# A hybrid decoder block in float32 parts: other rooms for w_out's first half rows, another order at the outset, and another closing norm

## The chip, the core and the metric

The kernel runs on one core of one Trainium2 chip. The metric is the device time of one execution in microseconds (us), lower is better. A core has a matrix engine (TensorE, in the profile PE for its products and PEld for its weight loads), a vector engine (VectorE, DVE), a scalar engine (ScalarE, ACT), a general engine (GpSimd, POOL) and a queue engine (SyncE, SP) that here only issues transfers. Each engine takes its own instructions in a fixed order. An instruction whose operand isn't there yet holds up all that stand behind it on the same engine, SP's transfers included.

## What is computed

One decoder block over 1024 tokens of width 1024, everything in float32:

```python
proj = x @ w_in                     # 1024 x 7168: q, f, i, out-gate, pool_v, gate_a, gate_b
a = HGRN2(q, f, i) -> per-head RMSNorm * sigmoid(og) -> @ w_a
b = per-group linear(causal_mean_w(pool_v) - pool_v) * pool_scale
mix = (sigmoid(gate_a) * a + sigmoid(gate_b) * b) @ w_out
x = LN(alpha * x + mix)
x = LN(alpha * x + relu(x @ w_up)**2 @ w_down)
```

`LN` takes a row's mean and variance over its 1024 columns, then multiplies by `g` and adds `b`.

## The kernel before, in words

**Products in three parts.** TensorE works on a rounded float32 format. Each operand is split into a high part (a cast on ScalarE) and a low part (a subtraction on VectorE), and a product is three matmuls of 128x128 by 128x512: high by high, high by low, low by high. Such a split of a weight row is `split` (L127, L128), of a weight block `w_part` (L250, L251), of an activation `split_into` (L132, L133), of a row of `w_out` `out_row` (L1181, L1182).

**Fewer products.** Every large product is cut into 2x2 blocks and done with seven block products instead of eight (names `a11`, `a12`, `s3`, `a22`, `s2`, `s1`, `s4` for the token operands, `p1` to `p7` for the products), with sums of blocks on VectorE before and after.

**Outset (L462 to L640).** SP first loads, in turns, 128-column pieces of `x`'s first 512 tokens (`load_x`, L488) and the rows of the first block `b11` of `w_in` (`load_block`, L505): pieces k=0, k=1, then k=2 and 3 together. TensorE runs `IDLE_PRODUCTS` = 12 products of the identity (L470), whose results nobody reads, then the transpose of the small parameters `prm` (L471, copied by L472). `first_tokens("a11")` transposes the sixteen 128x128 pieces of `x` (L171, four to a PSUM bank, one bank for each k), splits each bank into high and low (L132, L133) and copies it to `xt` (L188). `parts(b11)` splits the weight rows (L127, L128). Then `onto_chain` (L528 to L530) runs k by k, in each k over four banks `chain[c]`, the 48 matmuls of the first product; L561 copies the four banks away. The transposes of `a12`, the second half of `x`'s columns, stand between them, and `by_rows` follows with the next product (banks `ps_sc`, `ps_hg`).

**Rooms for loads in the stage of w_a.** The stage goes through two sets of two column pairs of `w_a` (`run(*(p[i : i + 1] for p in two))`). In the first set, `o_operand` (L672) loads each raw token operand into a 128x512 room got from `c_tile`: a ring of rooms named `c`, four in pool `ca`, and every third one in pool `wq`, which has two. `o_operand` is called for the seventh and last time ahead of the first set's sixth step of seven. In both sets `gated` (L1194 to L1198) loads two rows per result, a gate into one of ten rooms `ga` and a pooled row into one of two rooms `gb`. After the second set's second and third step, `out_rows_of` loads the eight half rows of `w_out` (columns 0 to 511), each through `loaded` (L660) into a room `gb` as well, and `out_row` splits it into an `act` tile. There are 28 `act` tiles; the split of `w_out`'s rows takes over those that the `a12` and `s3` token operands leave. L655 loads the other half rows of `w_out`. The product with `w_out` is `mix` (L114 to L116).

**End (from L1512).** The last block of the MLP's second product ends in two steps, `p3` (added to columns 512 to 1023, `nh` = 1) and `p2` (to columns 0 to 511, `nh` = 0), each over four row tiles c of 128 tokens, 12 matmuls a tile (L1492 to L1494). `add_to` (L1448) adds a finished bank onto the row tile on VectorE. `last_norm` then normalises it: for c < 3 with a sum on ScalarE (L1520, L1521), a sum of squares on ScalarE (L1522), a root (L1523), and on VectorE two passes over 1024 columns (L1528 multiplies by `g2`, L1531 multiplies by the reciprocal of L1529 and adds `b2`), and a transfer out (L1532). For c = 3, VectorE takes statistics of each half (L1260) and joins them (L1516), and both passes are cut into two halves, with a transfer each.

**What sets the order.** The kernel is written in a framework that traces it, then orders each engine's instructions by simulating the time, with program order as priority; `tc.high_priority(n)` raises it, and `tc.issue_after(ins)` puts an instruction behind `ins` in the order of its own engine, without a wait. A tile from a ring waits for the release of the tile that had the room. In one long stretch in the middle TensorE keeps program order; in the stages named above it doesn't.

Of the kernel before, what the change touches and what calls it, by code (L numbers as in the profile page):

```python
# [16 lines left out]
P = 128  # L17
S = 1024
D = 1024
# [23 lines left out]
IDLE_PRODUCTS = 12  # L43
# [9 lines left out]
def tile_hybrid_block(  # L53
# [36 lines left out]
    def nm(s):  # L90
        seq[0] += 1
        return f"{s}_{seq[0]}"
# [91 lines left out]
    def first_tokens(name, *tags):  # L184
        for kp in range(CH):
            ps, _ = transposed(r[:CH], HALF if name == "a12" else 0, kp, tags[kp % len(tags)])
            in_parts(name, kp, ps)
            A.copy(xt[name == "a12"][kp], ps)  # L188
# [272 lines left out]
    with tc.tile_pool(name="xr", bufs=8, side="right", reuse_waits="tile") as xr:  # L461
# [6 lines left out]

        for _ in range(IDLE_PRODUCTS):
            PE.matmul(ps[:, P : 2 * P], ident, ident, start=True, stop=True)  # L470
        PE.transpose(ps[:, 0:32], prm_r, ident[0:32, 0:32])  # L471
        V.tensor_copy(prm, ps[:, 0:32])  # L472
# [49 lines left out]
        def parts(rows):  # L522
            return [split(row, row_tile) for row in rows]
# [61 lines left out]
        first_tokens("a11", "tr", "tr", "hg", "hg")  # L585
        w = parts(b11[:2])
        for row, kp in zip(b11[2:], (1, 3)):
            lo_done, hi_done = made_kp["a11", kp]
            with tc.issue_after(lo_done), tc.issue_after(hi_done):
                w += parts([row])  # L590
# [11 lines left out]
        first_tokens("a12", "tr")  # L602
        onto_chain(w, "a11", True, copied(c11, c_late))
# [89 lines left out]
    with tc.tile_pool(name="tmp", bufs=1, side="right", reuse_waits="tile") as tmp:  # L693
# [527 lines left out]
        def out_rows_of(*ks):  # L1221
            for k in ks:
                out_row(loaded(w_out[k * P : (k + 1) * P, :HALF], mg_tile("gb", 2)), parts_of(act_tile))
# [288 lines left out]
    def last_norm(t):  # L1512

        mv = stat.tile([P, 4], F32, tag="lmv", name=nm("lmv"), bufs=4)
        if t == CH - 1:
            V.bn_aggr(mv[:, 0:2], st1[t])  # L1516
            A.activation(mv[:, 2:3], mv[:, 1:2], AF.Sqrt, bias=eps_ln)
        else:
            junk = dr.tile([P, D], F32, tag="junk", name=nm("junk"))
            A.activation(junk, r[t], AF.Copy, accum_out=mv[:, 3:4])  # L1520
            A.activation(mv[:, 0:1], mv[:, 3:4], AF.Copy, scale=-1.0 / D)  # L1521
            A.activation(junk, r[t], AF.Square, bias=mv[:, 0:1], accum_out=mv[:, 1:2])  # L1522
            A.activation(mv[:, 2:3], mv[:, 1:2], AF.Sqrt, bias=eps_ln, scale=1.0 / D)  # L1523
        n = 2 if t == CH - 1 else 1
        parts = [slice(i, i + D // n) for i in range(0, D, D // n)]
        for w in parts:
            op = ALU.subtract if t == CH - 1 else ALU.add
            V.scalar_tensor_tensor(r[t][:, w], r[t][:, w], mv[:, 0:1], g2[:, w], op, ALU.mult)  # L1528
        V.reciprocal(mv[:, 2:3], mv[:, 2:3])  # L1529
        for w, eng in zip(parts, (nc.sync, nc.scalar)):  # L1530
            V.scalar_tensor_tensor(r[t][:, w], r[t][:, w], mv[:, 2:3], b2[:, w], ALU.mult, ALU.add)  # L1531
            eng.dma_start(out=out2[t * P : (t + 1) * P, w], in_=r[t][:, w])  # L1532
# [37 lines left out]
    for i, c in ((0, 0), (0, 1), (1, 0), (0, 2), (1, 1), (1, 2), (0, 3), (1, 3)):  # L1570
        _, _, chain, fresh, (_, nh) = ends[i]
        ps = down_tile(ops[i], chain, fresh, c)
        with tc.high_priority(PRIO) if c == CH - 1 else nullcontext():
            add_to(c, nh, ps)
            if c == CH - 1:
                st1[c] = st1[c] if i else stat_tile()
                stats(r[c], nh, st1[c])
            if i:
                last_norm(c)
# [31 lines left out]
```

## Time and profile before

| | us |
|---|---|
| Median of 3 runs | 1447.27 |
| Lowest and highest of them | 1445.94, 1448.71 |
| The profiled execution's own time | 1449.68 |
| Its span, first to last instruction | 1447.9 |
| TensorE busy with products in the span | 1430.0 |
| VectorE, ScalarE, GpSimd busy | 1099.8, 757.6, 108.8 |

The profile is of one execution of its own, 2.41 us above the median of the three timed runs; 1.78 us of its time lie outside the span. A row of the timeline gives the start in us from the span's start, the duration, the engine, the line, the operation with out<-in, shapes and a count where equal instructions were merged, and in brackets the idle time of the engine before it with what ended it. Durations on TensorE overlap: a 128x512 product is shown with 0.39 us, but in a full stream one begins every 0.227 us. An SPq row is the issue of a transfer; its data arrive later.

### The profile page before, as it was taken

The page shows a single profiled execution, that of the slowest core. Times are in us where ns is not written, and L with a number is a line of the kernel's source. Part 1 is how long each engine was busy: PE and PEld are TensorE (multiplying, and loading weights), DVE is VectorE, ACT ScalarE, POOL GpSimd, SP SyncE. Part 2 cuts the span into 40 slices and gives each one's busy share as a digit, 9 for nine tenths or more (in the row PEclk, how much of TensorE's full clock was granted, in tenths as well). Part 3 has the DMA queues.
Part 4 walks back from the last instruction along what each step waited for, and adds up shares of the span by engine and source line. Part 5 has one row for each costly group of instructions (what it writes and reads, how often), then busy time and mean ns, then how long its engine had stood idle before and what let it go on. Part 6 is the DMA issues. An engine that isn't in the chain of part 4 may idle for free.

```text
span 1447.9 us, 20884 instructions
## 1 busy us (share of the span) xinstructions
PE 1430.0 (99%) x7377; PEld 1187.9 (82%) x7377; DVE 1099.8 (76%) x1807; ACT 757.6 (52%) x1383; POOL 108.8 (8%) x296
## 2 busy tenths in 40 slices
PE   9999999999999999999999999999999999999997
PEld 7888888888888888878788888888888888888886
DVE  5967877887797796579875697666666887777977
ACT  5445566666656645556433376555556443433535
POOL 0002011111212110100002100000000100000000
PEclk9999999999999999999999999999999999999999
DMA  7143254444444546799571225444457864445322
GB/s 269 61 137 94 84 131 145 109 126 145 110 124 132 136 126 190 211 318 321 173 245 62 88 73 189 160 160 157 143 174 254 289 244 148 149 145 173 118 72 117
DMA packets 186649, 228.15 MB, mean 158 GB/s; under 512 B 12176, under 2 KB 110512, under 8 KB 186544
## 3 DMA queue, kind: packets, MB, share of 16 engines
q1 hardware_dynamic: 179936, 210.81, 44.1%
q0 software_dynamic: 5824, 13.63, 4.5%
q10 hardware_dynamic: 784, 2.38, 0.6%
q8 instruction: 58, 0.95, 0.3%
q14 instruction: 47, 0.39, 0.1%
HBM read 149.70 MB, written 77.07 MB: 157 GB/s over the span
## 4 chain that ended last, share of the span: by engine, by line
PE 88%; DVE 6%; DMA 3%; issue 1%; ACT 1%; SPq 0%; DVEq 0%; ACTq 0%
PE ps_pj L213 15%; PE ps_pj L216 14%; PE ps_pj L215 14%; PE ps_pj L1493 4%; PE ps_pj L1494 4%; PE ps_pj L1492 4%; PE ps_pj L116 2%; PE ps_pj L115 2%; PE ps_pj L114 2%; PE ps_tr L1494 1%; PE ps_tr L1493 1%; PE ps_tr L1492 1%; DMA raw<-in_w_a_dram 1%; PE ps_hg L213 1%; PE ps_pj L529 1%
## 5 line engine op out<-in xcount | busy, mean ns | idle before, releaser
L213 PE MATMUL ps_pj<-act,w 128*128 128x512 f32 x1068 | 420.8, 394 | 4.4 <-ACT room L294 2.0
L215 PE MATMUL ps_pj<-act,w 128*128 128x512 f32 x1068 | 416.0, 390 | 0.0
L216 PE MATMUL ps_pj<-act,w 128*128 128x512 f32 x1068 | 415.9, 390 | 0.0
L250 ACT CAST w<-raw 128x512 fp32r<-128x512 f32 x303 | 187.6, 621 | 261.4 <-PE ps_pj L215 184.7
L251 DVE TENSOR_TENSOR w<-raw,w 128x512 fp32r<-128x512 f32 x303 | 206.9, 686 | 94.6 <-ACT w L250 93.0
L213 PEld LDWEIGHTS ps_pj<-act,w 128*128 128x128 f32 x1068 | 200.9, 188 | 48.7 <-DVE c L298 3.4
L216 PEld LDWEIGHTS ps_pj<-act,w 128*128 128x128 f32 x1068 | 200.9, 188 | 42.6
L215 PEld LDWEIGHTS ps_pj<-act,w 128*128 128x128 f32 x1068 | 200.9, 188 | 40.7
L1454 ACT CAST act<-act 128x1024 fp32r<-128x1024 f32 x66 | 66.9, 1050 | 110.1 <-issue 35.0
L1494 PE MATMUL ps_pj<-act,act 128*128 128x512 f32 x240 | 93.0, 389 | 0.0
L1493 PE MATMUL ps_pj<-act,act 128*128 128x512 f32 x240 | 93.0, 389 | 0.0
L1455 DVE TENSOR_TENSOR act<-act,act 128x1024 fp32r<-128x1024 f32 x66 | 79.4, 1219 | 17.5 <-ACT act L1454 16.5
L1492 PE MATMUL ps_pj<-act,act 128*128 128x512 f32 x240 | 92.5, 389 | 0.0
L298 DVE TENSOR_TENSOR c<-c,ps_pj 128x512 f32<-128x512 f32 x91 | 62.1, 682 | 34.4 <-PE ps_pj L216 33.6
L294 ACT COPY c<-ps_pj 128x512 f32<-128x512 f32 x92 | 53.5, 582 | 3.6 <-PE ps_pj L216 2.2
L1492 PEld LDWEIGHTS ps_pj<-act,act 128*128 128x128 f32 x240 | 45.0, 188 | 9.4
L1493 PEld LDWEIGHTS ps_pj<-act,act 128*128 128x128 f32 x240 | 45.0, 188 | 9.4
L1494 PEld LDWEIGHTS ps_pj<-act,act 128*128 128x128 f32 x240 | 45.0, 188 | 9.3
L303 DVE TENSOR_TENSOR raw<-raw,raw 128x512 f32<-128x512 f32 x43 | 29.6, 688 | 25.9 <-DMA raw<-in_w_in_dram 17.2
L1363 ACT ACTIVATE c<-c 128x512 f32<-128x512 f32 x61 | 38.6, 633 | 1.7
L1362 ACT ACTIVATE c<-c 128x512 f32<-128x512 f32 x46 | 29.1, 632 | 15.8 <-DVE c L298 15.8
L688 POOL DMA_DIRECT2D s<-og x28 | 25.0, 1164 | 138.7 <-DVE og L1105 138.7
(418 smaller groups left out, 2699.5 us busy)
## 6 DMA issues: line engine op xcount, KB each, us to landing
h<-c SPq DMA_DIRECT2D x106, 256.0 KB, 3.0
raw<-in_w_in_dram SPq DMA_DIRECT2D x100, 256.0 KB, 3.3
act<-h SPq DMA_DIRECT2D x78, 256.0 KB, 2.9
draw<-in_w_down_dram SPq DMA_DIRECT2D x16, 1024.0 KB, 7.9
raw<-in_w_up_dram SPq DMA_DIRECT2D x56, 256.0 KB, 3.0
hf<-h SPq DMA_DIRECT2D x34, 256.0 KB, 2.9
s<-og POOLq DMA_DIRECT2D x28, 256.0 KB, 6.2
v<-v SPq DMA_DIRECT2D x16, 256.0 KB, 3.3
```

The source lines that it names most:

```text
L213: PE.matmul(ps, wh[:, k], th, start=first and k == 0, stop=False, skip_group_check=True)
L215: PE.matmul(ps, wh[:, k], tl, start=False, stop=False, skip_group_check=True)
L216: PE.matmul(ps, wl[:, k], th, start=False, stop=k == CH - 1, skip_group_check=True)
L250: hi_of.append(A.copy(hi, src).ins)
L251: lo_of.append(V.tensor_sub(lo, src, f(hi)).ins)
L294: noted(A.copy(t, ps))
L298: V.tensor_add(t, t, ps)
L1454: A.copy(hi, src)
L1455: V.tensor_sub(lo, src, f(hi))
L1492: PE.matmul(ps, hh[:, w], wh, start=fresh and n == 0, stop=False, skip_group_check=True)
L1493: PE.matmul(ps, hh[:, w], wl, start=False, stop=False, skip_group_check=True)
L1494: PE.matmul(ps, hl[:, w], wh, start=False, stop=n == M - 1, skip_group_check=True)
```

## The change

There are three edits.

- **Rooms.** `out_rows_of` loads a half row of `w_out` into a room of `c_tile` instead of a room `gb`. Nothing else changes there.
- **Outset.** The twelve idle products become six and, behind the four transposes of k=0, three more. The order of TensorE is now spelled out: six products of k=0 onto chains 0 and 1, the transposes of k=1, six products of k=0 onto chains 2 and 3, the transpose of `prm`, six of k=1, the transposes of k=2 and k=3, six of k=1, then all of k=2, the transposes of `a12` placed behind these, and all of k=3. The casts of the weight rows are placed behind the splits of token pieces 0, 2 and 3, and the copies to `xt` later. The amount of products is the same but for the three idle ones.
- **End.** The last eight tiles are done in the order p3 c0, p3 c1, p2 c0, p2 c1, p3 c2, p2 c2, p3 c3, p2 c3 (before: p2 c1 stood behind p3 c2). Each adding instruction is now a `scalar_tensor_tensor` that also writes the row sums of its result. `end_norm` replaces `last_norm` for these four tiles: one small instruction makes the negative mean from the two sums, ScalarE takes the squares and the root, VectorE does the first pass over 1024 columns into another tile `z`, and the last pass is done in parts, for c = 3 in three (512, 256 and 256 columns) with a transfer each on SP, ACT and SP. `last_norm` stays for the four row tiles before, in its form for c < 3.

```diff
--- before.py
+++ after.py
@@ -40,7 +40,7 @@
 PRIO_WHOLE = 6000
 QUARTER = HALF // 2
 PRIO = 60
-IDLE_PRODUCTS = 12
+IDLE_PRODUCTS = (6, 3)
 WINDOWS = (2, 4, 8, 16)
 ALPHA = 2.0 ** 0.25
 LN_EPS = 1e-5
@@ -466,10 +466,11 @@
         prm = const.tile([P, 32], F32, name="prm")
         ps = ps_tile("hg", 2)
 
-        for _ in range(IDLE_PRODUCTS):
-            PE.matmul(ps[:, P : 2 * P], ident, ident, start=True, stop=True)
-        PE.transpose(ps[:, 0:32], prm_r, ident[0:32, 0:32])
-        V.tensor_copy(prm, ps[:, 0:32])
+        def idle_products(n):
+            for _ in range(n):
+                done = PE.matmul(ps[:, P : 2 * P], ident, ident, start=True, stop=True)
+            return done.ins
+
         g_col, pscale = prm[:, 16:24], prm[:, 24:32]
         lb = const.tile([P, 8], F32, name="lb")
         one_lb = const.tile([P, 8], F32, name="one_lb")
@@ -582,12 +583,55 @@
             A.copy(t, ps)
             put(0, 1, c, t)
 
-        first_tokens("a11", "tr", "tr", "hg", "hg")
-        w = parts(b11[:2])
-        for row, kp in zip(b11[2:], (1, 3)):
-            lo_done, hi_done = made_kp["a11", kp]
+        banks, w = [None] * CH, []
+
+        def first_turned(kp, tag):
+            banks[kp], done = transposed(r[:CH], 0, kp, tag)
+            in_parts("a11", kp, banks[kp])
+            return done
+
+        def row_parts(kp, behind):
+            lo_done, hi_done = made_kp["a11", behind]
             with tc.issue_after(lo_done), tc.issue_after(hi_done):
-                w += parts([row])
+                w.extend(parts([b11[kp]]))
+
+        def first_products(k, cs):
+            th, tl = xp["a11"][k][:, 0], xp["a11"][k][:, 1]
+            for t, wk in ((th, w[k][0]), (th, w[k][1]), (tl, w[k][0])):
+                for c in cs:
+                    done = PE.matmul(
+                        chain[c], t[:, c * P : (c + 1) * P], wk, start=k == 0 and t is th and wk is w[k][0],
+                        stop=k == CH - 1 and t is tl, skip_group_check=True,
+                    )
+            return done.ins
+
+        def bank_copied(kp):
+            A.copy(xt[0][kp], banks[kp])
+
+        idle_products(IDLE_PRODUCTS[0])
+        w += parts(b11[:1])
+        turned = first_turned(0, "tr")
+        with tc.issue_after(turned):
+            done = idle_products(IDLE_PRODUCTS[1])
+        with tc.issue_after(done):
+            done = first_products(0, (0, 1))
+        with tc.issue_after(done):
+            first_turned(1, "tr")
+            row_parts(1, 0)
+            first_products(0, (2, 3))
+            done = PE.transpose(ps[:, 0:32], prm_r, ident[0:32, 0:32]).ins
+        V.tensor_copy(prm, ps[:, 0:32])
+        with tc.issue_after(done):
+            done = first_products(1, (0, 1))
+        with tc.issue_after(done):
+            first_turned(2, "hg")
+            row_parts(2, 2)
+            first_turned(3, "hg")
+            bank_copied(0)
+            row_parts(3, 3)
+            first_products(1, (2, 3))
+        for kp in range(1, CH):
+            bank_copied(kp)
         with behind_parts("a11"):
             V.tensor_max(lb, prm[:, 0:8], prm[:, 8:16])
             V.tensor_sub(e01[:, 0:8], prm[:, 0:8], lb)
@@ -599,8 +643,13 @@
             V.tensor_scalar(one_lb, lb, -1.0, 1.0, ALU.mult, ALU.add)
             g_neg = e01[:, 0:8]
             V.tensor_scalar_mul(g_neg, g_col, -1.0)
-        first_tokens("a12", "tr")
-        onto_chain(w, "a11", True, copied(c11, c_late))
+        done = first_products(2, range(CH))
+        with tc.issue_after(done):
+            first_tokens("a12", "tr")
+        first_products(3, range(CH))
+        with tc.high_priority(PRIO):
+            for c in range(CH):
+                copied(c11, c_late)(c, chain[c])
         with behind_parts("a11"):
             w = parts(b21)
         second_tokens("s3", "tr")
@@ -1220,7 +1269,7 @@
 
         def out_rows_of(*ks):
             for k in ks:
-                out_row(loaded(w_out[k * P : (k + 1) * P, :HALF], mg_tile("gb", 2)), parts_of(act_tile))
+                out_row(loaded(w_out[k * P : (k + 1) * P, :HALF], c_tile), parts_of(act_tile))
 
         names = ("a11", "a12", "s3", "a22", "s2", "s1", "s4", None)
         two = [a_pair(p) for p in range(2)]
@@ -1512,24 +1561,27 @@
     def last_norm(t):
 
         mv = stat.tile([P, 4], F32, tag="lmv", name=nm("lmv"), bufs=4)
-        if t == CH - 1:
-            V.bn_aggr(mv[:, 0:2], st1[t])
-            A.activation(mv[:, 2:3], mv[:, 1:2], AF.Sqrt, bias=eps_ln)
-        else:
-            junk = dr.tile([P, D], F32, tag="junk", name=nm("junk"))
-            A.activation(junk, r[t], AF.Copy, accum_out=mv[:, 3:4])
-            A.activation(mv[:, 0:1], mv[:, 3:4], AF.Copy, scale=-1.0 / D)
-            A.activation(junk, r[t], AF.Square, bias=mv[:, 0:1], accum_out=mv[:, 1:2])
-            A.activation(mv[:, 2:3], mv[:, 1:2], AF.Sqrt, bias=eps_ln, scale=1.0 / D)
-        n = 2 if t == CH - 1 else 1
-        parts = [slice(i, i + D // n) for i in range(0, D, D // n)]
-        for w in parts:
-            op = ALU.subtract if t == CH - 1 else ALU.add
-            V.scalar_tensor_tensor(r[t][:, w], r[t][:, w], mv[:, 0:1], g2[:, w], op, ALU.mult)
+        junk = dr.tile([P, D], F32, tag="junk", name=nm("junk"))
+        A.activation(junk, r[t], AF.Copy, accum_out=mv[:, 3:4])
+        A.activation(mv[:, 0:1], mv[:, 3:4], AF.Copy, scale=-1.0 / D)
+        A.activation(junk, r[t], AF.Square, bias=mv[:, 0:1], accum_out=mv[:, 1:2])
+        A.activation(mv[:, 2:3], mv[:, 1:2], AF.Sqrt, bias=eps_ln, scale=1.0 / D)
+        V.scalar_tensor_tensor(r[t], r[t], mv[:, 0:1], g2, ALU.add, ALU.mult)
         V.reciprocal(mv[:, 2:3], mv[:, 2:3])
-        for w, eng in zip(parts, (nc.sync, nc.scalar)):
-            V.scalar_tensor_tensor(r[t][:, w], r[t][:, w], mv[:, 2:3], b2[:, w], ALU.mult, ALU.add)
-            eng.dma_start(out=out2[t * P : (t + 1) * P, w], in_=r[t][:, w])
+        V.scalar_tensor_tensor(r[t], r[t], mv[:, 2:3], b2, ALU.mult, ALU.add)
+        nc.sync.dma_start(out=out2[t * P : (t + 1) * P, :], in_=r[t])
+
+    def end_norm(t, mv, z, *parts):
+
+        y, junk = r[t], dr.tile([P, D], F32, tag="junk", name=nm("junk"))
+        V.tensor_scalar(mv[:, 2:3], mv[:, 0:1], mv[:, 1:2], -1.0 / D, ALU.add, ALU.mult)
+        A.activation(junk, y, AF.Square, bias=mv[:, 2:3], accum_out=mv[:, 3:4])
+        A.activation(mv[:, 3:4], mv[:, 3:4], AF.Sqrt, bias=eps_ln, scale=1.0 / D)
+        V.scalar_tensor_tensor(z, y, mv[:, 2:3], g2, ALU.add, ALU.mult)
+        V.reciprocal(mv[:, 3:4], mv[:, 3:4])
+        for w, eng in zip(parts, (nc.sync, nc.scalar, nc.sync)):
+            V.scalar_tensor_tensor(z[:, w], z[:, w], mv[:, 3:4], b2[:, w], ALU.mult, ALU.add)
+            eng.dma_start(out=out2[t * P : (t + 1) * P, w], in_=z[:, w])
 
     w_scope.close()
     dr = ctx.enter_context(tc.tile_pool(name="dr", bufs=1, side="right", reuse_waits="tile"))
@@ -1567,16 +1619,17 @@
 
     ends = steps[-2:]
     ops = [down_operands(NBLK - 1, name, slot) for name, slot, *_ in ends]
-    for i, c in ((0, 0), (0, 1), (1, 0), (0, 2), (1, 1), (1, 2), (0, 3), (1, 3)):
+    ends_last = slice(0, HALF), slice(HALF, HALF + QUARTER), slice(HALF + QUARTER, D)
+    flat = [t.rearrange("p a b -> p (a b)") for t in (*t2, t1, t2[0])]
+    sums = [stat.tile([P, 4], F32, tag="lmv", name=nm("lmv"), bufs=4) for _ in range(CH)]
+    for i, c in ((0, 0), (0, 1), (1, 0), (1, 1), (0, 2), (1, 2), (0, 3), (1, 3)):
         _, _, chain, fresh, (_, nh) = ends[i]
         ps = down_tile(ops[i], chain, fresh, c)
         with tc.high_priority(PRIO) if c == CH - 1 else nullcontext():
-            add_to(c, nh, ps)
-            if c == CH - 1:
-                st1[c] = st1[c] if i else stat_tile()
-                stats(r[c], nh, st1[c])
+            y = r[c][:, nh * HALF : (nh + 1) * HALF]
+            V.scalar_tensor_tensor(y, y, 1.0, ps, ALU.mult, ALU.add, accum_out=sums[c][:, i : i + 1])
             if i:
-                last_norm(c)
+                end_norm(c, sums[c], flat[c], *(ends_last if c == CH - 1 else (slice(0, D),)))
 
 
 # ---- launch: one core; inputs and outputs as the reference has them ----
```

## The prediction, made before the changed kernel was run

> **What bounds the kernel now.** The page's first lines, then TensorE's own waits.
>
> ```profile
> span 1447.9 us, 20884 instructions
> PE 1430.0 (99%) x7377; PEld 1187.9 (82%) x7377; DVE 1099.8 (76%) x1807; ACT 757.6 (52%) x1383; POOL 108.8 (8%) x296
> ```
>
> TensorE (PE) is the bound: of 1447.9 us it leaves 17.9 idle, 9.1 of them behind its last product (1438.81, below). The edits take no product of the block away, so they can only win idle time, products that nobody reads, and time at a lowered clock. The waits (us in total, times, longest) say which idle time has one cause:
>
> ```profile
> PE ps_pj L213 <- ACT room L294: 2.0, 1, 2.0
> PE ps_pj L213 <- DVE c L298: 2.0, 2, 1.1
> PE ps_sc L171 <- DMA x<-in_x_dram: 1.4, 1, 1.4
> ```
>
> The first row is the rooms' stage, the last the outset.
>
> **Rooms.** The timeline around the wait (SP, ACT, PE), and behind it busy times of L213's products, then the granted clock:
>
> ```profile
> 719.41 0.33 SPq L660 DMA_DIRECT2D gb<-in_w_out_dram  x1
> ...
> 723.30 0.62 ACT L1181 CAST act<-gb 128x512 fp32r<-128x512 f32 x1 [2.53 <-DMA gb<-in_w_out_dram]
> 723.83 0.61 ACT L250 CAST w<-raw 128x512 fp32r<-128x512 f32 x1
> 724.35 0.58 ACT L294 COPY room<-ps_pj 128x512 f32<-128x512 f32 x1
> ...
> 724.98 0.50 PE L213 MATMUL ps_pj<-act,w 128*128 128x512 f32 x1 [2.04 <-ACT room L294]
> ...
> 727.30 0.62 ACT L1181 CAST act<-gb 128x512 fp32r<-128x512 f32 x1 [0.62 <-DMA gb<-in_w_out_dram]
> ```
>
> ```profile
> 726.00:729.10 3.10, 1.49 (x3) 0.75 (x3) 0.50 0.66 214
> ```
>
> ScalarE stood 2.53 us before the cast of a row of w_out whose transfer SP had issued only 3.9 us earlier; the copy that frees TensorE's bank stood two places behind. TensorE lost 2.04 us, and then ran at a granted clock of 0.50 for 3.1 us, which is 1.6 us more. The issue was late because it needed one of two rooms gb, which the pooled rows use too. After the change it needs a room c. There are six, and their last user, the token operands, is done by then:
>
> ```profile
> 678.07 0.62 ACT L132 CAST act<-c 128x512 fp32r<-128x512 f32 x1 [0.58 <-DMA c<-s]
> ...
> 706.69 0.62 ACT L1181 CAST act<-gb 128x512 fp32r<-128x512 f32 x1
> ```
>
> So six of eight rows can be issued from about 679, 27 us ahead of the first cast at 706.69, and the other two once the first casts are done, well before the last cast at 727.30. Nothing is added: the same eight transfers, casts and subtractions. The gain is 2.04 + 1.6 = **3.6 us**; what is late next is the act tile that a cast needs, which TensorE itself gives back, and in the trace the casts at 723 and 727 wait for transfers alone. Bounds: 0 if a new wait of this size takes its place; 2.0 if the stall in the timed runs mostly doesn't lower the clock.
>
> **Outset.** PE, then ACT and DVE, then the time to landing of x's first two pieces, issued at 0.82 and 1.85:
>
> ```profile
> 1.66 4.88 PE L470 MATMUL ps_hg<-ident 128*128 128x128 f32 x24 [1.66 <-POOL inv_n L150]
> 6.38 0.93 PE L171 MATMUL ps_tr<-ident,x 128*128 128x128 f32 x7
> 7.24 0.24 PE L471 MATMUL ps_hg<-ident,prm_r 32*128 32x32 f32 x1
> 9.10 0.66 PE L171 MATMUL ps_sc<-ident,x 128*128 128x128 f32 x4 [1.36 <-DMA x<-in_x_dram]
> 9.95 0.48 PE L528 MATMUL ps_pj<-w,act 128*128 128x512 f32 x1
> ...
> 10.96 0.40 PE L528 MATMUL ps_pj<-w,act 128*128 128x512 f32 x1
> ```
>
> ```profile
> 5.08 0.62 ACT L127 CAST w<-b 128x512 fp32r<-128x512 f32 x1 [1.51 <-DMA b<-in_w_in_dram]
> 5.73 0.69 DVE L128 TENSOR_TENSOR w<-b,w 128x512 fp32r<-128x512 f32 x1 [5.73 <-ACT w L127]
> ...
> 10.75 0.63 ACT L127 CAST w<-b 128x512 fp32r<-128x512 f32 x1
> ```
>
> ```profile
> x<-in_x_dram SPq DMA_DIRECT2D x1, 256.0 KB, 2.8
> ...
> x<-in_x_dram SPq DMA_DIRECT2D x1, 256.0 KB, 4.5
> ```
>
> The first piece of x landed at 0.82 + 2.8 = 3.6 us and the second at 1.85 + 4.5 = 6.4, but the first useful product began at 9.95, behind twelve idle products, sixteen transposes and a wait for the third piece. The idle products' pace comes from L470's weight loads (the second count) in two stretches:
>
> ```profile
> 3.66:5.66 2.00, 2.00 (x12) 2.00 (x10) 1.00 0.82 240
> 5.86:6.36 0.50, 0.50 (x7) 0.49 (x5) 1.00 0.88 314
> ```
>
> Ten passes in 2.0 us, then five in 0.5: 0.2 us and 0.1 us. TensorE starts at half pace and doubles it at about 5.7 us, 4 us after its first product (the clock column, 1.00 throughout, doesn't show that; the pace does). Twelve products were 24 passes, so six are 12 and end near 1.66 + 2.6 = 4.3. The four transposes of k=0 follow, 0.11 us each at full pace (seven in 0.93 with the last one's tail), 0.22 at half: done by 5.2. Three idle products take 1.3 at half pace, to 6.4 or a little sooner. Meanwhile ScalarE casts the weight row at 5.08 and the piece of x behind it by 6.2, and VectorE's low parts are ready at 6.4 and 7.0, ahead of the third product and the fifth. So useful products begin near 6.4, not 9.95. Twelve transposes (1.3 us) and that of prm (0.2) still stand to be done, so the chain is ahead by 9.95 - 6.4 - 1.5 = 2.05. With 0.15 for more changes between transposes and products I take **1.9 us**. I find no wait further on: k=1's transposes come at 7.8, its piece landed at 6.4; k=2 and 3 come near 11.3, theirs landed by 9.1; the weight rows of k=2 and 3 are wanted from 13.5, and theirs was there by 10.75, where the first was cast. Next late are the rows of b12:
>
> ```profile
> 13.11 1.73 SPq L505 DMA_DIRECT2D act<-in_w_in_dram  x2
> ```
>
> ```profile
> act<-in_w_in_dram SPq DMA_DIRECT2D x2, 512.0 KB, 10.6
> ```
>
> ```profile
> 25.96 2.49 DVE raw L610 x4
> ```
>
> They were issued at 13.11 and near 14.5, so they land near 23.7 and 25.1; VectorE reads the first at 25.96 and the second half a group, 1.2, later, some 2.1 us after each landing. Moved 1.9 earlier, it just finds them. So this gain ends at about 2.1. From below: if the pace doubled one stretch of 3.1 to 3.4 us later (the length of the slow stretch at 726), products from 6.4 to about 9.2 would run at half pace and 1.4 us be lost, which leaves 0.5.
>
> [...]
>
> **End.** The last product, then VectorE's instructions, the last issue, and ScalarE's for the tile before:
>
> ```profile
> 1438.42 0.39 PE L1494 MATMUL ps_tr<-dx,dx 128*128 128x512 f32 x1
> ```
>
> ```profile
> 1439.74 1.28 DVE L1531 SCALAR_TENSOR_TENSOR act<-act,lmv,ln 128x1024 f32<-128x1024 f32 x1
> ...
> 1443.23 0.15 DVE L1529 RECIPROCAL lmv<-lmv 128x1 f32<-128x1 f32 x1
> 1443.42 1.41 DVE L1531 SCALAR_TENSOR_TENSOR act<-act,lmv,ln 128x512 f32<-128x512 f32 x2
> ```
>
> ```profile
> 1435.70 1.16 ACT L1522 ACTIVATE junk<-act,lmv 128x1024 f32<-128x1024 f32 x1
> 1436.76 0.18 ACT L1522 ACTIVATION_READ_ACCUMULATOR junk<-act,lmv 128x1 f32 x1
> 1436.98 0.29 ACT L1523 ACTIVATE lmv<-lmv,eps_ln 128x1 f32<-128x1 f32 x1
> ...
> 1444.87 0.35 ACTq L1532 DMA_DIRECT2D out_dram<-act  x1
> ```
>
> ```profile
> L842 DVE SCALAR_TENSOR_TENSOR f<-ps_tr,prm,f 128x512 f32<-128x512 f32 x2 | 1.5, 742 | 0.0
> ```
>
> TensorE ends at 1438.42 + 0.39 = 1438.81, and the last transfer is issued 6.06 us later. In between stands the last pass of the tile before (1.28), which the new order of tiles moves forward. New sum, with 0.04 for each hop between engines or dependent steps (1436.98 less 1436.94): hop 0.04; the add as a scalar_tensor_tensor out of PSUM, 0.74 by L842; the row sum's read-out, which no row shows on VectorE, 0 to 0.18 by ScalarE's, and I take 0.18; mean 0.04 + 0.15 by L1529; hop, square, read-out and root 0.04 + 1.57; hop, reciprocal, hop 0.23; pieces of 512, 256 and 256 columns 0.67 + 0.40 + 0.48 (two of 512 take 1.41, so one begins 0.67 after the other and takes 0.74; by the slope from 1.28 for 1024 one of 256 takes 0.48); hop 0.03. That is 4.57, so **1.5 us** are won. The first pass over 1024 columns (1.28) lies beside ScalarE's 1.57 and would cost nothing. From 1444.87 to the end stay 3.07 us; the last transfer has half the bytes, for which I count nothing. Bounds: 1.9 without the read-out and with a transfer 0.2 shorter; 0.3 if the tile before still puts its 1.28 in front. That tile's last product now ends two tiles, 24 x 0.227 = 5.4 us, before the end, and its norm takes 3.0 by the sum above up to the last pass, and 1.28 for that, so it should be out of the way.
>
> [...]
>
> **Sum.** 3.6 + 1.9 + 1.5 = 7.0 us. The profiled execution would take 1449.68 - 7.0 = 1442.7. The timed runs lay 2.4 below it: 1447.27 - 7.0 = **1440.3**. By the bounds the three give between 0.8 and 7.6.
>
> **Rivals.**
>
> - *The stall in the rooms' stage is only replaced*: ScalarE still stands before a cast, now for an act tile. For it: each cast takes a tile that TensorE must leave first. Against: 2.53, the wait that hit TensorE, was for a transfer. Price: only 3.4 won, 1443.9. Chance 0.17.
> - *The pace doubles a stretch later* at the outset: 7.0 - 1.4, 1441.7. Chance 0.10.
> - *The end wins less*: the 1.28 of the tile before stays in front, 1441.6, or an add that sums takes twice its 0.74, 1441.0. Chance 0.07.
> - *Slower: SP is blocked by its own early loads.* Eight rows want six rooms; the seventh waits on SP for the first cast, and pooled and gate rows queue behind it. SP has been held so:
>
> ```profile
> 678.78 10.06 SPq L660 DMA_DIRECT2D gb<-pb  x3
> ```
>
>   Three issues took 10.06 us, and TensorE didn't wait. If the same block came at 700, where each pooled row is soon wanted, TensorE would lose up to 10.1 and 1.6 for the clock, less 3.4 for the other edits: 8.3 slower, 1455.6. It decides once the unhidden block passes 3.4 - 1.6 + 2.9 = 4.7. Against: the order is simulated, so that issues which can't start stand late. Chance 0.08.
> - *The change doesn't do what it says*: the simulated order moves other instructions, and a wait of some 2 us comes or goes elsewhere (L213 behind L298, 2.0 in two). 1438.3 or, with the edits' gain eaten by several, about 1447. Chance 0.06 each.
>
> The forecast itself has 0.46. Its own range is 1439.0 to 1442.5. For 8 in 10 I take 1437.5 to 1444.5, which leaves out the blocked queue, the eaten gain and the tail of the replaced stall. A measurement of this kernel tells about 0.2%, 2.9 us, from no change. Faster by more: the forecast, both small rivals, most of the first, and the good half of the last, 0.83. Within: 0.09. Slower: 0.08.
>
> **What would show it.** Rooms: no TensorE wait on L294 near 720, clock 1.00 throughout, the w_out rows issued by 700. Outset: the first 128x512 product near 6.4, the by_rows products (banks sc, hg) beginning 1.9 us earlier. End: last issue 4.6 us behind the last product, not 6.1. The forecast is wrong if another TensorE wait of over 2 us stands in these places.

## The result and the profile after

| | before | after |
|---|---|---|
| Median, us (20 runs each, side by side) | 1448.35 | 1444.36 |
| Lowest and highest, us | 1445.94, 1450.72 | 1442.76, 1446.25 |
| The profiled execution, us | 1449.68 | 1444.12 |
| Its span, us | 1447.9 | 1442.4 |

The ratio is 0.9973, with a 95% interval of 0.9967 to 0.998: the change makes the kernel 4.0 us faster (2.9 to 4.8). The forecast was 7.0 us and 1440.3. Of the 4.1 us that separate 1440.3 from 1444.36, 3.0 are missing gain, and 1.1 come from the starting point: 20 runs put the median of before at 1448.35, where three had put it at 1447.27.

The two profiled executions differ by more than the medians do, 5.5 us of span. Where these 5.5 lie is read from instructions that both kernels have. First TensorE's waits of 0.5 us and over, of after:

```profile
PE ps_pj L213 <- DVE c L298: 2.1, 3, 0.9
PE ps_hg L471 <- POOL inv_n L150: 1.7, 1, 1.7
PE ps_tr L114 <- DVE f L891: 1.0, 1, 1.0
PE ps_tr L171 <- DVE x L198: 0.7, 1, 0.7
PE ps_sc L529 <- DVE c L566: 0.5, 1, 0.5
```

The 2.0 us behind L294 and the 1.4 us behind x's transfer are gone; 0.7 and 0.5 at the outset stand behind VectorE (in before it was one wait of 0.5). Now the timeline of TensorE at four places, before and then after: the first product of the scores, the last product of the pooling, the first transpose for the MLP behind w_a's stage, the last product of all.

```profile
137.31 0.46 PE L1027 MATMUL sc<-tF,tD 128*32 128x32 f32 x32
...
645.93 0.39 PE L116 MATMUL ps_tr<-w,og 128*128 128x512 f32 x1
...
777.97 0.38 PE L171 MATMUL ps_tr<-ident,r 128*128 128x128 f32 x2
```

```profile
136.30 0.46 PE L1076 MATMUL sc<-tF,tD 128*32 128x32 f32 x32
...
645.55 0.39 PE L116 MATMUL ps_tr<-w,og 128*128 128x512 f32 x1
...
773.63 0.38 PE L171 MATMUL ps_tr<-ident,r 128*128 128x128 f32 x2
...
1434.22 0.39 PE L1543 MATMUL ps_tr<-dx,dx 128*128 128x512 f32 x1
```

Up to the scores after is 1.0 us ahead (outset). From there to 645 it loses 0.6 again, in a part that the diff doesn't touch. From 645 to the transposes it needs 128.1 us where before needed 132.0: 4.0 us (rooms). The MLP takes the same time within 0.1. Behind the last product, which ends at 1434.22 + 0.39 = 1434.61, 7.8 us are left where before had 9.1: 1.3 us (end). 1.0 - 0.6 + 4.0 - 0.1 + 1.3 = 5.6, the 5.5 but for rounding. In this pair of executions the rooms brought what the forecast said of them, 3.6 and more. The experiments ask whether they do so every time.

### The profile page after: what moved, and what is told of

Its sections match the earlier page's. It is cut to its first block, busy times and chain, and to the rows that moved or that the text cites. A ratio compares the mean times of both kernels' runs of the same rounds, so it can differ in the third digit from the quotient of the medians.

```text
span 1442.4 us, 20884 instructions
## 1 busy us (share of the span) xinstructions
PE 1428.1 (99%) x7371; PEld 1185.5 (82%) x7371; DVE 1099.0 (76%) x1816; ACT 753.7 (52%) x1376; POOL 108.4 (8%) x296
## 4 chain that ended last, share of the span: by engine, by line
PE 92%; DVE 4%; DMA 2%; ACT 1%; issue 1%; SPq 0%; DVEq 0%; ACTq 0%
PE ps_pj L213 15%; PE ps_pj L215 15%; PE ps_pj L216 15%; PE ps_pj L1542 4%; PE ps_pj L1541 4%; PE ps_pj L1543 4%; PE ps_pj L114 2%; PE ps_pj L115 2%; PE ps_pj L116 2%; PE ps_tr L1541 2%; PE ps_tr L1542 2%; PE ps_tr L1543 2%; PE ps_hg L216 1%; PE ps_sc L216 1%; PE ps_hg L215 1%; PE ps_sc L215 1%
## 5 line engine op out<-in xcount | busy, mean ns | idle before, releaser
L294 ACT COPY c<-ps_pj 128x512 f32<-128x512 f32 x92 | 53.4, 581 | 3.3 <-PE ps_pj L216 1.8
```

What stands on the lines that cost most here:

```text
L294: noted(A.copy(t, ps))
```

## The experiments

**One edit at a time, and before against itself.** Four kernels ran on one chip; the median of before there was 1447.39 (35 runs). The first is the kernel before, unchanged, which shows how far a profile and a ratio stray by themselves.

> The kernel before once more, unchanged. Theory A, that the fall of the clock behind the 2.0 us wait near 722 us comes in some executions only: the mean granted clock of its runs is 0.997 in some and 0.998 to 0.999 in others, and the runs lie apart by up to 1.7 us for it. Rival B, that wait and fall come every time: 0.997 in all. The time is that of the kernel before within 0.1% in either case.

The rooms alone:

```diff
-                out_row(loaded(w_out[k * P : (k + 1) * P, :HALF], mg_tile("gb", 2)), parts_of(act_tile))
+                out_row(loaded(w_out[k * P : (k + 1) * P, :HALF], c_tile), parts_of(act_tile))
```

> Only the rooms of w_out's first half rows are changed. Theory A (the wait of 2.0 us goes every time, the 1.6 us of halved clock behind it only where it came): 2.0 to 3.0 us faster than before. Rival B (both come every time in the kernel before): 3.6 us faster. If the stall were only replaced by another: within 1 us of before. The profile has no wait of TensorE on L294 between 700 and 730 us under A and B.

The outset alone (the first four hunks of the diff, the rest as before):

> Only the outset is changed. Theory A: 1.9 us ahead where the by_rows products begin, but only about 1.0 us ahead from 33 us on, since VectorE's chain from 23 to 30 us moves by 1.1 us and TensorE waits for it, so about 1.0 us faster than before. Rival B, that the whole lead is kept: 1.9 us faster. Rival C, that the pace of TensorE doubles late in timed runs: 0.5 us faster or less.

The end alone (the last two hunks, the rest as before):

> Only the end is changed. From the last product to the last transfer's issue 4.4 us in place of 6.06, but from that issue to the end 3.4 in place of 3.07, since the third piece stands behind the first on SP's queue. Theory A: 1.3 us faster than before. Rival B, the term as forecast: 1.5 to 1.9 us faster.

| kernel | median, us (runs) | ratio to before, 95% interval | of 1447.4 us |
|---|---|---|---|
| before again | 1447.98 (12) | 1.0004 [0.9994, 1.0015] | +0.6 |
| rooms alone | 1447.06 (11) | 0.9993 [0.9981, 1.0005] | -1.0 |
| outset alone | 1445.95 (12) | 0.9990 [0.9981, 0.9999] | -1.4 |
| end alone | 1446.43 (11) | 0.9989 [0.998, 0.9998] | -1.6 |

The last column is the ratio's share of 1447.4. By it the three add up to -4.0, what the change does as a whole; the medians alone would give -0.3, -1.4 and -1.0, together -2.7, so the sum isn't known to better than 1 or 2 us. Outset and end are near the forecast of 1.9 and 1.5, and their intervals (-2.8 to -0.1, -2.9 to -0.3) don't tell theory A from rival B. The rooms, forecast at 3.6, show 1.0, less than theory A's 2.0 to 3.0 as well; their interval (-2.8 to +0.7) leaves 3.6 out, but neither no gain nor the lower part of theory A.

The profiles say why. The windows of 640 to 770 us, TensorE's busy time first; before, then before again, the same program:

```profile
640.00:770.00 130.00, 127.96 (x557) 105.41 (x556) 107.84 (x178) 63.42 (x114) 1.90 (x3) 0.99 0.72 235
```

```profile
640.00:770.00 130.00, 129.94 (x573) 107.15 (x572) 109.83 (x182) 65.11 (x115) 3.48 (x3) 1.00 0.72 238
```

TensorE stood idle for 0.06 us in the second, not 2.04. ScalarE stood before the same cast, that of the sixth half row, in every kernel without the rooms edit (timeline of ScalarE, the wait in brackets; before again, end alone, outset alone):

```profile
721.12 0.62 ACT L1181 CAST act<-gb 128x512 fp32r<-128x512 f32 x1 [1.80 <-DMA gb<-in_w_out_dram]
```

```profile
723.67 0.62 ACT L1181 CAST act<-gb 128x512 fp32r<-128x512 f32 x1 [2.37 <-DMA gb<-in_w_out_dram]
```

```profile
718.47 0.62 ACT L1230 CAST act<-gb 128x512 fp32r<-128x512 f32 x1 [1.33 <-DMA gb<-in_w_out_dram]
```

The five profiles without the edit, with the time from the pooling's last product to the transposes for the MLP beside them (the last kernel is described below; all times in us):

| profile | ScalarE's wait before the sixth cast | TensorE idle, 640 to 770 | pooling to transposes |
|---|---|---|---|
| before | 2.53 | 2.04 | 132.04 |
| end alone | 2.37 | 1.31 | 129.98 |
| the changed kernel with the old rooms | 1.94 | 0.00 | 128.08 |
| before again | 1.80 | 0.06 | 128.48 |
| outset alone | 1.33 | 0.02 | 128.39 |

The rooms did hold the transfers up in each of these five executions, but TensorE lost up to 0.4 us where ScalarE waited 1.94 us or less, and 1.9 and 4.0 (of which 1.6 are the lowered clock) where it waited 2.37 and 2.53. So TensorE seems to have work of its own for some 2 us of this wait. The wait's length alone doesn't set the loss, though: between 2.37 and 2.53 the wait at the sixth cast grows by 0.16 and the idle time by 0.73, and what else decides wasn't followed. In end alone the granted clock was 1.00 over the window in spite of its 1.31 us; of these five only the execution that was profiled for before had the fall. In all eight profiles with the rooms edit the same stretch takes 128.08 us. Against that the five lose between 0.0 and 4.0 us, 1.3 in the mean. (The idle time alone shows less, because the durations on TensorE overlap: a product is shown with 0.39 us where one begins every 0.227, so a gap of up to 0.16 between two of them isn't counted.) The window of after:

```profile
640.00:770.00 130.00, 130.00 (x575) 107.59 (x573) 110.96 (x183) 64.19 (x114) 4.90 (x4) 1.00 0.71 238
```

The clock of all executions points the same way, as theory A of before again had it. Of 94 executions of the kernel before, on three chips, 9 had a mean granted clock of 0.996 or 0.997; they took 1451.2 us in the mean, 3.7 more than the rest. The profiled one was of these (0.997). Of 32 of the changed kernel none was. But a mean doesn't say where the clock fell, and the edit doesn't rule such executions out: one of 11 with the rooms alone had 0.997 (1451.03 us), and one of 9 of the last variant below (1445.31).

**Less of the change, or more.** Four kernels on another chip, where before had a median of 1448.15 (32 runs): the changed kernel again, and two variants of it and both together. The last tile's last pass in two pieces in place of three:

```diff
-    ends_last = slice(0, HALF), slice(HALF, HALF + QUARTER), slice(HALF + QUARTER, D)
+    ends_last = slice(0, HALF), slice(HALF, D)
```

and the transposes of a12's first three pieces ahead of the next block's products (`turned_kp` holds each piece's last transpose):

```diff
-        by_rows(w, "a12", take_p2)
+        with tc.issue_after(turned_kp["a12", 2]): by_rows(w, "a12", take_p2)
```

> The changed kernel once more, beside the variants of this call. 4.0 us faster than before (0.27%), with no wait of TensorE on L294 near 720 us, and 7.8 us from the end of the last product to the end of the span.

> The changed kernel with the last pass of the last row tile in two pieces of 512 columns, a transfer each on SP and ACT, in place of three. Theory A, that the third piece's transfer is what is late (its issue 0.13 us later by three starting costs instead of two, its landing 2.43 us after the issue instead of 2.05): from the last product to the end 7.3 us in place of 7.8. Rival B, that the smaller last transfer wins: 7.9 to 8.0.

> The changed kernel with the by_rows products of a12 placed behind the transposes of a12's third piece, so that these come at about 19.9 us in place of 22.1. Theory A, that the lead of the outset is given back because those transposes come late and VectorE's chain behind them with them: TensorE's waits between 27 and 30 us fall from 1.3 us to 0.8 or less, and the score products of the first half start 0.4 to 0.8 us earlier than in the changed kernel, against the first product. Rival B, that the landing of b12's rows at 24.3 and 25.7 us binds: the waits stay at 1.1 or more.

> Both variants together: two pieces at the end, a12's third transposes ahead. Under both theories A 0.9 to 1.3 us faster than the changed kernel, about 5 us faster than the kernel before; under both rivals B the time of the changed kernel within 0.3 us.

| kernel | median, us (runs) | ratio to before, 95% interval |
|---|---|---|
| after again | 1444.20 (12) | 0.9972 [0.9961, 0.9982] |
| two pieces | 1443.73 (12) | 0.9975 [0.9966, 0.9985] |
| a12 early | 1443.66 (12) | 0.9972 [0.9961, 0.9983] |
| both | 1444.65 (9) | 0.9976 [0.9966, 0.9987] |

All four are the same within what the runs can tell, 0.1%. The variants together aren't 0.9 to 1.3 us faster than the changed kernel, as both theories A had it. The third piece of the last pass is worth nothing that shows: from the last product's end to the end of the span it is 7.6 us in two pieces and 7.8 with three, which is neither theory's number. The early transposes moved what they were to move, and won little. Of the 5 us from 26 to 31, TensorE was busy for 3.72 in after and for 4.26 in a12 early. They won 0.54 us of idle time there, but 0.35 of transposes now stand ahead of the products, so 0.2 is left, where theory A had 0.4 to 0.8. VectorE was busy for all of the 5.00 in both: TensorE waited 0.74 and 0.55 us for it in after, and 0.7 in a12 early, where another 0.4 stand behind ScalarE.

**The rooms from the other side, and made worse.** On a third chip, where before had 1448.07 (15 runs), two kernels were timed. The changed kernel with `mg_tile("gb", 2)` back in `out_rows_of`:

> The changed kernel with w_out's half rows back in the two rooms gb; the outset and the end stay as changed. Theory A (the stall in the rooms' stage comes in some executions only; the edit is worth 1.0 to 1.6 us in the mean): 1445.3 to 1446.0 us, ratio to the kernel before 0.9980 to 0.9985. Theory B (it is worth the 3.6 us forecast in every execution): about 1448, ratio 0.9997. Theory C (it is worth nothing, and all of the gain is from the other two edits): 1444.3, ratio 0.9972. In the profile A and C allow TensorE's idle time from 640 to 770 us to be anything from 0 to 2; B asks for about 2 and a lowered clock behind it. ScalarE's waits for rows of w_out (1.3 to 2.5 us before the cast) return by all theories.

It took 1445.02 (11 runs), ratio 0.9981 [0.9972, 0.999]. That is theory A's number; the 0.9997 of a full 3.6 is outside the interval, and the changed kernel's 0.9972 and 0.9973 are at its lower edge. So the edit is worth 0.0008 to 0.0009, **1.2 to 1.3 us**, beside the other two, about as much as the 1.0 it was worth alone. Taken by themselves the times of both experiments would just allow theory C, that it is worth nothing; against C stand the stretches of the profiles, 1.3 us in the mean. The profile had no TensorE wait from 640 to 770 at all. The kernel before with `mg_tile("gb", 1)` for both kinds of rows:

> The kernel before with one room gb in place of two, for w_out's half rows and for the pooled rows. Theory A (the two rooms limit the issue of these transfers, ScalarE waits for them, and TensorE waits where ScalarE's wait is over some 2 us): the row after a cast is issued later still, ScalarE's waits grow to 3 us or more for several of the eight rows, TensorE's idle time from 640 to 770 us goes from 0.1 - 2.0 to 5 us or more in every execution, and the time rises by 4 to 15 us (ratio 1.003 to 1.010). Theory B (the 2.0 us wait in the profile of before was a transfer that happened to be slow, whatever the rooms): idle time there stays under 2 and the time within 1.5 us of before (ratio 0.999 to 1.001).

It took 1475.26 (4 runs), ratio 1.0194 [1.018, 1.0208]: 27 us slower, theory A, and far beyond the 4 to 15 that it gave. TensorE's window, its longest wait, and the SP rows behind it:

```profile
640.00:770.00 130.00, 111.40 (x481) 90.21 (x480) 91.42 (x148) 54.81 (x98) 1.09 (x2) 0.94 0.59 191
```

```profile
PE ps_pj L114 <- ACT act L121: 16.1, 1, 16.1
```

```profile
737.41 8.54 SPq L660 DMA_DIRECT2D gb<-in_w_out_dram  x3
750.84 16.71 SPq L660 DMA_DIRECT2D gb<-pb  x6
```

With one room a row can be issued only when the row before it has landed and been read: three half rows took SP 8.54 us and six pooled rows 16.71, and TensorE stood 16.1 us for the last of them, with a granted clock of 0.94 over the window. That is the queue of my blocked-SP rival. The time was lost behind the pooled rows, though, and hardly behind the half rows of w_out: ScalarE waited 2.58 and 2.75 us for two of these ahead of 717, and TensorE was busy all through 640 to 720. So theory A's 2 us hold for the place of the sixth cast in before, and not for any wait of ScalarE. With six rooms `c` it didn't arise: SP issued six of the eight rows between 678 and 684 and two at 707, and ScalarE's casts were done by 715.5, with no wait for a transfer (SP, then ScalarE, of after):

```profile
678.21 1.02 SPq L709 DMA_DIRECT2D c<-in_w_out_dram  x2
...
707.18 1.57 SPq L709 DMA_DIRECT2D c<-in_w_out_dram  x2
```

```profile
704.50 1.67 ACT L1230 CAST act<-c 128x512 fp32r<-128x512 f32 x3
707.07 0.62 ACT L1230 CAST act<-c 128x512 fp32r<-128x512 f32 x1
713.26 2.18 ACT L1230 CAST act<-c 128x512 fp32r<-128x512 f32 x4
```

**What doubles TensorE's pace.** Two variants of the changed kernel's outset, one execution of each. Each idle product replaced by two transposes, and then only two idle products in all:

```diff
-            for _ in range(n):
-                done = PE.matmul(ps[:, P : 2 * P], ident, ident, start=True, stop=True)
+            for _ in range(2 * n):
+                done = PE.transpose(ps[:, P : 2 * P], ident, ident)
```

> The changed kernel with each idle product at the outset replaced by two transposes of the identity, whose results are not read either. Theory A (the doubling of TensorE's pace comes 3 to 6 us after its first instruction of any kind, seen at 4.7 to 7.3 us so far): doubled by 7.5 us, first products of 128x512 near 6.4 or a little sooner and 0.227 us apart by 8, by_rows at 19.8 to 20.6. [...]

```diff
-IDLE_PRODUCTS = (6, 3)
+IDLE_PRODUCTS = (1, 1)
```

> The changed kernel with one idle product ahead of the transposes of k=0 and one behind, in place of six and three. Theory A (the doubling of the pace needs only time since TensorE began, not that it be kept busy): doubled by 7.5 us all the same, by_rows at 19.5 to 20.6, time within 0.5 us of the changed kernel. Theory B (TensorE must be kept busy for about 4 us first): TensorE is idle for some 2 us ahead of the first useful product, the pace doubles only at 8 to 11 us, and by_rows comes 1 to 2 us later, at 21 to 22.5.

They took 1445.34 and 1444.57, one run each, from which nothing follows. TensorE's timeline does tell. First with transposes, then with few idle products:

```profile
1.66 2.82 PE L471 MATMUL ps_hg<-ident 128*128 128x128 f32 x12 [1.66 <-POOL inv_n L150]
4.28 1.06 PE L171 MATMUL ps_tr<-ident,x 128*128 128x128 f32 x4
5.13 0.93 PE L471 MATMUL ps_hg<-ident 128*128 128x128 f32 x6
6.01 1.66 PE L602 MATMUL ps_pj<-w,act 128*128 128x512 f32 x6
```

```profile
3.65 1.11 PE L171 MATMUL ps_tr<-ident,x 128*128 128x128 f32 x4 [1.20 <-DMA x<-in_x_dram]
4.56 0.64 PE L471 MATMUL ps_hg<-ident 128*128 128x128 f32 x2
5.54 2.93 PE L602 MATMUL ps_pj<-w,act 128*128 128x512 f32 x6 [0.34 <-ACT act L132]
8.26 1.05 PE L171 MATMUL ps_tr<-ident,x 128*128 128x128 f32 x4
8.97 2.03 PE L602 MATMUL ps_pj<-w,act 128*128 128x512 f32 x6
10.93 0.25 PE L622 MATMUL ps_hg<-ident,prm_r 32*128 32x32 f32 x1
11.10 1.65 PE L602 MATMUL ps_pj<-w,act 128*128 128x512 f32 x6
```

With nothing but transposes ahead of it, the first group of six products takes 1.66 us, full pace, and the next block begins at 19.73, as in after (19.83). So in this execution the transposes did the work of the idle products. The second kernel asks whether the time since TensorE's first instruction is enough: TensorE was idle for 1.20 and 0.34 us, the first six products took 2.93 (2.72 to the next start, one every 0.45) and the second six 2.03 (1.96 to the next start), and only the third group, at 11.10, ran at full pace throughout (1.65, 1.49 to the next start). The pace doubled within the second group, near 10 by an estimate: two products of 0.45 behind 8.97. The next block began at 21.24, 1.4 us later than after's 19.83. One execution each could be a matter of chance, since the changed kernel's own outset scatters too: TensorE's first group of six, in after and in after again,

```profile
5.91 1.66 PE L602 MATMUL ps_pj<-w,act 128*128 128x512 f32 x6
```

```profile
6.38 2.12 PE L602 MATMUL ps_pj<-w,act 128*128 128x512 f32 x6
```

took 1.66 and 2.12 us, and in after again the next block began at 20.55. But over the seven profiles with nine idle products the group took 1.62 to 2.12, and 2.93 lies outside that. So the time since TensorE's first instruction doesn't do it alone: with less work and two gaps ahead of the products the pace doubled later.

## Why the prediction was right and wrong

The direction, the mechanisms and the places were right, but the forecast of 7.0 us was 3.0 too high, most of it in one term. 1444.36 lies outside the forecast's own 1439.0 to 1442.5, and inside 1437.5 to 1444.5, by 0.14 us. That is luck: the wider range reached so far for the rival of a stall that is only replaced (1443.9), and that rival didn't come.

**Rooms: 3.6 forecast, 1.0 to 1.3 measured. This is the step that failed.** The signs named were there, but for one: no TensorE wait on L294, clock 1.00, casts 12 us earlier, nothing late in their place. Of the eight half rows six were issued by 700 and two at 707, which cost nothing. What failed is "the gain is 2.04 + 1.6", two numbers of the one execution that was profiled, subtracted from all of them. That execution took 1449.68, 2.4 us above the median that I had, and I carried the distance along as an offset (1447.27 less 7.0), where it was a hint that the stall itself was part of the distance. Five profiles without the edit have 2.04, 1.31, 0.06, 0.02 and 0.00 us of idle TensorE from 640 to 770, and one in five has the 1.6 us for the clock; the whole stretch is 0.0 to 4.0 us longer than with the edit, 1.3 in the mean. The timed runs show 1.0 and 1.2 to 1.3. Five profiles are few for a mean, but in none of them but the first was the whole 3.6 lost. My lower bound asked whether the clock falls in the timed runs; that the stall itself might mostly be absent I didn't ask, though the bound of 0 covered it for another reason. The rival that a new wait replaces the stall is refuted by the rows of after.

**Outset: 1.9 forecast, 1.4 (0.1 to 2.7) in the runs and 1.0 in the profile.** The useful products began at 5.91 (forecast near 6.4), and the next block at 19.83, where before had 21.84: 2.0 ahead, as forecast (the block's first products, before and after):

```profile
21.84 0.39 PE L528 MATMUL ps_sc<-w,act 128*128 128x512 f32 x1
```

```profile
19.83 0.39 PE L529 MATMUL ps_sc<-w,act 128*128 128x512 f32 x1
```

By the scores 1.0 was left. In five profiles with this outset the scores begin between 135.89 and 136.92, in five with that of before between 137.31 and 137.66, so 1.2 is left in the mean. What I put as "this gain ends at about 2.1" ended earlier, and not at the rows of b12 but at VectorE. VectorE and then TensorE, of after:

```profile
23.36 0.69 DVE L133 TENSOR_TENSOR act<-ps_tr,act 128x512 fp32r<-128x512 f32 x1 [3.39 <-ACT act L132]
24.27 0.69 DVE L133 TENSOR_TENSOR act<-ps_tr,act 128x512 fp32r<-128x512 f32 x1 [0.22 <-ACT act L132]
24.88 2.49 DVE L659 TENSOR_TENSOR raw<-raw,act 128x512 f32<-128x512 f32 x4
27.28 0.68 DVE L198 TENSOR_TENSOR x<-xt,ps_tr 128x512 f32<-128x512 f32 x1
...
28.48 0.68 DVE L566 TENSOR_TENSOR c<-c,ps_sc 128x512 f32<-128x512 f32 x1
```

```profile
28.02 0.66 PE L171 MATMUL ps_tr<-ident,x 128*128 128x128 f32 x4 [0.74 <-DVE x L198]
29.22 0.50 PE L529 MATMUL ps_sc<-w,act 128*128 128x512 f32 x1 [0.55 <-DVE c L566]
```

VectorE's four sums of rows begin at 24.88, where before had them at 25.96: 1.1 earlier, not 2.0. It works without a gap from 24.88, and TensorE waits 0.74 and 0.55 us for it. Ahead of the sums stand the low parts of a12's last two pieces (23.36 and 24.27), and VectorE stood idle 3.39 us for the first of these, whose transposes TensorE does behind ten of the next block's products. I looked for what comes late among the transfers and among the operands of the 48 products, and not along VectorE's own queue behind them. The rows of b12 come close behind: by their issue and their time to landing they were there near 24.3 and 25.7, so the sums could have begun 0.4 us sooner at most. The early transposes moved the waits by half a microsecond and gave most of it back, so which order would win the rest stays open.

The rival of a pace that doubles later didn't come in after, where the first group of six took 1.66 us. It came in part in after again (2.12, the next block 0.7 us later) and in a12 early (2.05), so it is a draw of each execution, too, at half of the 1.4 us that I gave it. The kernel with few idle products was 1.4 late, with two idle products and gaps of 1.20 and 0.34 us ahead of the useful ones; with transposes in place of all idle products the next block wasn't late (19.73).

**End: 1.5 forecast, 1.35 in the profile of after, 1.6 (0.3 to 2.9) in the runs.** VectorE and the last issue on SP, of after:

```profile
1434.65 0.69 DVE L1630 SCALAR_TENSOR_TENSOR act<-act,ps_tr 128x512 f32<-128x512 f32 x1
1435.26 0.08 DVE L1630 DVE_READ_ACCUMULATOR act<-act,ps_tr 128x1 f32 x1
```

```profile
1439.00 0.33 SPq L1584 DMA_DIRECT2D out_dram<-act  x1
```

The last issue comes 1439.00 - 1434.61 = 4.39 us behind the last product (forecast 4.57). The row sum's read-out takes 0.08 and not 0.18. The rival of an add that takes twice its 0.74 has no run that shows it: the last add takes 0.69 in after, in end alone and in two pieces. The tile before is out of the way. What I had counted as nothing is the transfer: from the last issue to the end it is 1442.39 - 1439.00 = 3.39 us, where before had 3.07 with twice the bytes. That is the 0.3 by which a faster chain gave no more than 1.35. It isn't a price of the small third piece: end alone and the changed kernel with the old rooms end with the same piece, and there it takes 3.0 to 3.1 us, not the 3.4 that I expected of end alone, and the end is 1.7 us shorter than that of before. In these two the last piece landed 2.1 us after its issue, in after 2.4, and the list of queues in after has a row that theirs lack, one transfer of the kind "instruction" in the window of the last pieces:

```profile
q14 instruction: 1, 0.01, 0.2%
```

Whether that transfer holds the last piece up wasn't tested; with two pieces, where no such row stands in the window, the time behind the last issue is 3.3 us as well.

**Rivals.** SP's block (slower) didn't come, since six rooms were free in time; the price of such a block was right in kind, as the kernel with one room shows (16.1 us of TensorE in one wait, where I gave up to 10.1). The order of other instructions did change something: the stretch from the first score product to the pooling's last took 0.6 us longer in after than in before. But it took between 507.4 and 511.1 us over fourteen profiles, after again 508.1, so nothing can be laid on the change there.

## What to carry to other kernels

A stall behind a transfer in one profile may be a draw of that execution (here 2.04 us in one, 0.00 to 1.31 in four others): take a second profile of the unchanged kernel, or compare the profiled execution's time with the median, before its whole length is put into a sum. A lead of one engine can be lost in the next engine's queue (here TensorE's 2.0 us at the next block were 1.0 at the scores, behind VectorE), so it has to be followed through the queues of all engines until it is spent or safe. A ring of rooms that cost 1.0 to 1.3 us with two rooms cost 27 us, 2%, with one; compare the time from issue to release (with one room three issues took SP 8.54 us) with the time between uses.

## What the runs showed of the hardware

A wait of TensorE of 2.04 us was followed by 3.1 us at a granted clock of 0.50 (before); one of 0.94 us (end alone) was not, the clock stayed at 1.00. At the outset the pace doubled before 6 us with nine idle products (in after, where the first six useful products, at 5.91, took 1.66 us; in after again only within the first six, which began at 6.38 and took 2.12) and with transposes in their place (at 6.01, 1.66), and near 10 with two: there the second group of six products, at 8.97, took 1.96 us to the next start, where after's takes 1.56, and the 0.40 more are an estimate of two products at the first group's 0.45 in place of 0.227. The same program on the same data lost between 0.06 and 2.04 us in the rooms' stage, from a transfer that was waited for 1.80 or 2.53 us.
